# Feed-forward block on one core: a second Strassen level for product 4 of block 0, its result added to the stored rows by accumulating DMA

One core of one Trainium2 chip. The metric is the device time of one execution in microseconds (us), as the median of several runs; lower is better.

## The reference

```python
batch, m, k, h, n = 16, 512, 768, 3072, 768
def reference(x, w1, b1, w2):            # all float32
    y = np.matmul(x, w1) + b1
    y = 0.5 * y * (1.0 + erf(y / np.sqrt(2.0)))
    return np.matmul(y, w2)
```

The 8192 rows are worked in eight blocks of 1024. Each matmul is done in float16 by a Strassen-Winograd scheme: 7 products of half-size matrices in place of 8, with sums of operands made beforehand (VectorE, "DVE") and sums of products afterwards (DVE and ScalarE, "ACT"). TensorE ("PE") does the matmuls. Transfers between the chip's memory and DRAM (DMA) are issued from the queues of SyncE ("SP", the sync queue), ScalarE and GpSimd ("POOL"). "Nested" products apply the same scheme once more, so that one product becomes 7 sub-products of half the rows, half the inner dimension and half the columns.

## The kernel before

Blocks 0 and 1 do the second matmul mostly by plain products; blocks 2 to 7 do it nested throughout, with W2 operands that blocks 0 and 1 have computed and stored to DRAM (`w2s`) on the way: some as plain blocks of W2 ("raw"), most as sums of two blocks ("W2 sums"). In block 0, four units (`Unit2`, 128 row pairs each) do products 1, 3, 4, 5, 6, 7 plain, and one nested unit (`UnitH`) does product 2 for all rows. Four nested units follow each other, (0,2), (1,1), (1,4), (1,2) as (block, product), then four "lean" units of block 1.

```python
class Unit2:
    def mm(self, p, dst, first, c0, c1):
        if p == 2 or self.lean and p in (1, 4):        # these are nested
            return
        ...
        for c in range(c0, c1):                        # 12 matmuls of 384 columns
            nc.tensor.matmul(out=dst[:, 0:N2], lhsT=a, rhs=w[:, :, c, :], ...)
    def left_done(self, row, bank):
        if row == 0:
            if not self.lean:                          # upper left half: kept on chip for product 2
                nc.scalar.copy(out=self.rows(par02), in_=bank[:, 0:N2])
            return
        ...

class UnitH(Unit3):
    def __init__(self, g, sb, m):
        ...
        self.add = {0: par02, 1: par1}[self.sb] if self.p == 2 else None   # added by DVE
    def mm(self, q, dst, first, c0, c1):
        for c in range(NQ):                            # 6 x 2 matmuls of 192 columns
            for t in range(2):
                nc.tensor.matmul(out=dst[:, t * N4:(t + 1) * N4], lhsT=a, rhs=self.w[q][:, c, :], ...)

def split_w2(p, t, q=None):       # four W2 sums of product p into buffers spare[t], each then stored
    ...
            tt(t[n], a, b, SUB)                                    # DVE
            puts.append([LAG[0], lambda eng: put(n, t[n], eng)])   # store two slots later (SP queue)
```

The instruction streams are interleaved by hand: a period runs the first products of unit i and the last ones of unit i-1, with seven slots between them in which DVE work and transfers are put. DVE takes its instructions in the order of the program, so one that waits holds up those behind it (for 3.6 us in the result below).

```python
def fill_mm2_one(sb, U, slot):                         # block 0, unit U
    ...
        if U == 0:
            for p in (1, 2, 3, 5, 6, 7, 4):
                raw_w2(p)                              # 3 raw W2 tiles each, stored two per slot
            for p, t in ((6, (0, 1, 2, 3)), (1, (4, 5, 0, 1)), (4, (2, 3, 4, 5)), (2, (0, 1, 2, 5))):
                split_w2(p, t)
def fill_hyb(sb, m, slot):                             # nested units
    ...
    if m == 1 and slot == 6:
        split_w2(7, (6, 7, 8, 9))
        split_w2(5, (6, 7, 8, 9))
```

## Time and profile before

| | before |
|---|---|
| median of 3 runs | 852.22 us (851.93 to 852.35) |
| span of the profiled run | 850.3 us |
| PE instructions | 6468 matmuls and 6468 weight loads |
| first matmul of block 0's units to the first full unit of block 2 ("the stretch") | 120.53 to 230.23 us: 109.70 us |
| end of PE's last matmul to the end of the span ("the tail") | 3.75 us |

What bounds the kernel is shown in the prediction below. First the busy time of each engine in two windows, then how many W2 sums and raw tiles are stored in each (count, size, median us from issue to landing):

```profile
core 0: us, PE busy (x) PEld busy (x) DVE busy (x) ACT busy (x) POOL busy (x), PEclk, DMA share, GB/s
120.50:158.00 37.50, 37.50 (x229) 22.31 (x228) 33.18 (x46) 9.95 (x21) 0.00 (x0) 1.00 0.81 280
158.00:232.00 74.00, 74.00 (x617) 54.97 (x616) 55.48 (x80) 16.30 (x35) 13.30 (x24) 1.00 0.84 234
```

```profile
w2s<-arena SPq DMA_DIRECT2D x30, 288.0 KB, 3.8
...
w2s<-arena SPq DMA_DIRECT2D x13, 288.0 KB, 6.2
```

On average the transfers have about a fifth of the time to spare in both windows, but from 180 to 210 us their share is already 1.01 to 1.17 (three windows of 10 us). And these are the transfers of the last 10 us:

```profile
out_dram<-arena SPq DMA_DIRECT2D x5, 384.0 KB, 2.5
out_dram<-arena SPq DMA_DIRECT2D x1, 192.0 KB, 2.4
...
out_dram<-arena ACTq DMA_DIRECT2D x1, 96.0 KB, 2.3
```

### The profile page before, as it was taken

The numbers are of one execution on the slowest core, as the hardware profiler recorded it, in microseconds if no ns is written. First come the engines' busy times: TensorE is split into PE (matmuls) and PEld (weight loads), VectorE is DVE, ScalarE is ACT, GpSimd is POOL, SyncE is SP. The second block draws the span as 40 slices with busy tenths as digits, with TensorE's granted clock in tenths as the row PEclk, the third lists the DMA queues.
The fourth block names the chain that finished last, engine by engine and source line by source line (L and its number), as shares of the span: only waits on it lengthen the run. The fifth ranks groups of instructions, "written<-read, shape, count | busy, mean of one in ns | idle before, by whom it ended". The sixth has DMA issues, their size and how long they took to land.

```text
span 850.3 us, 16583 instructions
## 1 busy us (share of the span) xinstructions
PE 843.9 (99%) x6468; PEld 571.3 (67%) x6468; DVE 671.1 (79%) x1132; ACT 423.6 (50%) x692; POOL 89.9 (11%) x147
## 2 busy tenths in 40 slices
PE   8999999999999999999999999999999999999998
PEld 5444445697544897449964499645995469944798
DVE  5766679877757998679976799667996689956998
ACT  4777762221277413773147822587216771277611
POOL 5021100022200002000020000200002100010000
PEclk9999999999999999999999999999999999999999
DMA  9998697679899699977999689995999949984398
GB/s 226 193 281 182 159 194 256 232 203 262 314 278 207 199 336 363 307 166 246 337 372 283 134 287 335 373 286 112 314 345 349 293 102 331 354 312 170 101 303 290
DMA packets 144066, 220.82 MB, mean 260 GB/s; under 512 B 61916, under 2 KB 84884, under 8 KB 143988
## 3 DMA queue, kind: packets, MB, share of 16 engines
q1 hardware_dynamic: 117536, 178.36, 67.0%
q0 software_dynamic: 26272, 41.30, 21.7%
q8 instruction: 50, 0.82, 0.4%
q14 instruction: 28, 0.23, 0.1%
q10 hardware_dynamic: 180, 0.11, 0.0%
HBM read 182.07 MB, written 47.87 MB: 270 GB/s over the span
## 4 chain that ended last, share of the span: by engine, by line
PE 98%; DMA 1%; ACT 0%; DVE 0%; SPq 0%; issue 0%; ACTq 0%
PE bY L411 21%; PE bY L516 15%; PE bX L411 14%; PE bX L516 10%; PE bW L411 7%; PE bZ L411 7%; PE bZ L516 5%; PE bW L516 5%; PE bY L456 5%; PE bZ L456 2%; PE bW L456 2%; PE bY L603 1%; PE bX L603 1%; PE bX L456 1%; DMA arena<-in_x_dram 1%; PE bX L778 0%
## 5 line engine op out<-in xcount | busy, mean ns | idle before, releaser
L208 DVE TENSOR_TENSOR arena<-arena 128x1536 f16<-128x1536 f16 (+6 forms) x634 | 405.9, 671 | 6.6 <-PE bW L456 1.0
L411 PEld LDWEIGHTS <-arena 128*128 128x128 f16 x1974 | 192.5, 98 | 224.3 <-issue 0.6
L516 PEld LDWEIGHTS <-arena 128*128 128x128 f16 x3528 | 292.1, 98 | 8.3 <-issue 0.4
L411 PE MATMUL bY<-arena 128*128 128x512 f16 x846 | 214.4, 379 | 0.1
L629 DVE TENSOR_TENSOR arena<-bY,arena 128x512 f32<-128x512 f32 (+1 forms) x102 | 69.4, 680 | 119.0 <-PE bY L411 91.9
L516 PE MATMUL bY<-arena 128*128 128x192 f16 x1500 | 138.3, 246 | 0.0
L411 PE MATMUL bX<-arena 128*128 128x512 f16 x564 | 138.2, 379 | 0.0
L622 ACT COPY bY<-bX 128x512 f32<-128x512 f32 (+1 forms) x144 | 79.1, 549 | 118.2 <-DVE arena L565 81.5
L427 ACT ACTIVATE arena<-arena,b1t 128x1024 f16<-128x1024 f32 x94 | 108.0, 1149 | 52.0 <-DVE arena L657 52.0
L642 ACT COPY arena<-bW 128x512 f32<-128x512 f32 (+1 forms) x148 | 81.5, 551 | 92.2 <-PE bW L516 44.3
L516 PE MATMUL bX<-arena 128*128 128x192 f16 x1020 | 93.1, 246 | 0.1
L657 DVE TENSOR_TENSOR arena<-bZ,arena 128x512 f32<-128x512 f32 (+1 forms) x102 | 69.2, 679 | 22.1 <-PE bZ L411 18.2
L411 PE MATMUL bZ<-arena 128*128 128x512 f16 x282 | 76.2, 379 | 0.0
L411 PE MATMUL bW<-arena 128*128 128x512 f16 x282 | 76.2, 379 | 0.0
L548 POOL DMA_DIRECT2D out_dram<-arena x42 | 30.5, 728 | 409.1 <-DVE arena L653 375.0
L432 ACT ACTIVATE arena<-bX,b1t 128x512 f16<-128x512 f32 x94 | 64.0, 681 | 10.5 <-PE bX L411 10.5
L673 ACT COPY bZ<-bY 128x512 f32<-128x512 f32 (+1 forms) x58 | 30.8, 532 | 75.6 <-PE bY L456 30.0
L456 PEld LDWEIGHTS <-arena 128*128 128x128 f16 x480 | 46.9, 98 | 31.0 <-issue 0.2
L432 ACT ACTIVATE arena<-bY,b1t 128x512 f16<-128x512 f32 x94 | 63.4, 674 | 0.0
L516 PE MATMUL bZ<-arena 128*128 128x192 f16 x504 | 48.5, 246 | 0.0
L516 PE MATMUL bW<-arena 128*128 128x192 f16 x504 | 48.4, 246 | 0.0
L316 POOL DMA_DIRECT2D arena<-in_x_dram x60 | 32.3, 546 | 152.3 <-DMA arena<-arena 142.0
(62 smaller groups left out, 413.9 us busy)
## 6 DMA issues: line engine op xcount, KB each, us to landing
arena<-w2s SPq DMA_DIRECT2D x300, 288.0 KB, 4.6
arena<-w1s SPq DMA_DIRECT2D x72, 672.0 KB, 7.0
out_dram<-arena POOLq DMA_DIRECT2D x46, 384.0 KB, 7.4
w2s<-arena SPq DMA_DIRECT2D x49, 288.0 KB, 4.1
arena<-in_x_dram POOLq DMA_DIRECT2D x60, 192.0 KB, 7.3
w1s<-arena SPq DMA_DIRECT2D x12, 672.0 KB, 6.1
arena<-in_w_dram POOLq DMA_DIRECT2D x17, 384.0 KB, 7.5
out_dram<-arena SPq DMA_DIRECT2D x9, 384.0 KB, 2.6
```

The source lines that it names most:

```text
L208: nc.vector.tensor_tensor(out=o, in0=a, in1=b, op=op)
L316: nc.gpsimd.dma_start(out=xhs[t], in_=xr[:, sb * 8 + t, :])
L411: nc.tensor.matmul(out=dst[:, 0:RH], lhsT=w1_op(self.wt, slot)[:, c, :], rhs=a[:, c, :], start=first and c == 0, stop=c == self.C - 1, ski ...
L427: nc.scalar.activation(out=self.G[1][:, hi, :, :], in_=self.tmp, func=GELU, bias=b1t[:, 2 * hi + 1:2 * hi + 2])
L432: nc.scalar.activation(out=self.G[0][:, hi, row, :], in_=bank[:, 0:RH], func=GELU, bias=b1t[:, 2 * hi:2 * hi + 1])
L456: nc.tensor.matmul(out=dst[:, 0:N2], lhsT=a, rhs=w[:, :, c, :], start=first and c == 0, stop=c == self.C - 1, skip_group_check=True)
L516: nc.tensor.matmul(out=dst[:, t * N4:(t + 1) * N4], lhsT=a, rhs=w[:, c, :], start=first and c == 0 and t == ts[0], stop=c == NQ - 1, skip_ ...
L622: nc.scalar.copy(out=bY[u.g % 2][:, 0:u.F], in_=bX[u.g % 2][:, 0:u.F])
L629: nc.vector.tensor_tensor(out=u.c22(), in0=bY[u.g % 2][:, 0:u.F], in1=w[:, 0:u.F], op=ADD)
L642: nc.scalar.copy(out=w[:, 0:u.F], in_=bW[:, 0:u.F])
L657: nc.vector.tensor_tensor(out=u.c12(), in0=bZ[:, 0:u.F], in1=w[:, 0:u.F], op=ADD)
L673: nc.scalar.copy(out=bZ[:, 0:u.F], in_=bY[u.g % 2][:, 0:u.F])
```

## The change

The intent: nest product 4 of block 0 as well, which saves an eighth of its columns. Both nested products of block 0 then add to rows that the plain units have stored already: their partial sums go out by an accumulating DMA, so no DVE add is needed. The operand sums of product 4 need a place, so buffers move, and the order of the W2 sums changes. Cut to its core:

```diff
-    o_stage = o_wt + 2 * N + PAR
+    o_stage = o_wt + PAR
...
-    hyb_w = {2: {7: stage[0], 5: stage[1], 6: stage[2], 4: stage[5]}, ...
+    w4 = {7: stage[6], 5: stage[4], 6: stage[5], 4: wb_at(o_x0 + W2_N)}
+    hyb_w = [{7: stage[3], 5: stage[0], 6: stage[1], 4: stage[2]}, w4, w4,
+             {7: stage[0], 5: stage[1], 6: stage[2], 4: stage[3]},
+             {7: stage[6], 5: stage[4], 6: stage[5], 4: stage[1]}]
...
-        HYBRID = ((0, 2), (1, 1), (1, 4), (1, 2))
+        HYBRID = ((0, 2), (0, 4), (1, 4), (1, 1), (1, 2))
...
-                if p == 2 or self.lean and p in (1, 4):
+                if p in (2, 4) or self.lean and p == 1:
...
             def finish(self):
...
+                    if self.sb:
+                        nc.gpsimd.dma_start(out=o, in_=d)
+                    else:
+                        nc.gpsimd.dma_start(out=o, in_=d, accum_op=ADD)
...
         def fill_mm2_one(sb, U, slot):
-                    for p, t in ((6, (0, 1, 2, 3)), (1, (4, 5, 0, 1)), (4, (2, 3, 4, 5)), (2, (0, 1, 2, 5))):
-                        split_w2(p, t)
-            drain(slot)
+                    w4 = (6, 4, 5, 3)
+                    split_w2(4, w4, ns=(5, 6, 4))
+                    split_w2(1, (0, 1, 2, 6))
+                    split_w2(2, (3, 0, 1, 2))
+                    split_w2(4, w4, ns=(7,))
+            drain(slot, 3 if U == 0 and slot > 1 else 0)
...
         def fill_hyb(sb, m, slot):
-            drain(slot)
+            drain(slot, int(slot > 1))
...
+            if m == 2 and slot == 1:
+                load_w2s(3, (5, 6, 7, 4))
+            if m == 3 and slot == 1:
+                load_w2s(4, (5, 6, 7))
+            if m == 4 and slot == 1:
+                load_w2s(4, (4,))
+            if m == 2 and slot == 5:
+                for p in (6, 7):
+                    split_w2(p, (7, 8, 9, 10))
...
         def fill_lean(sb, k, slot):
-                split_w2(3, (1, 2, 3, 4))
+                for p in (5, 3):
+                    split_w2(p, (0, 2, 3, 5))
```

More of the change, by code (lines that the diff above doesn't have):

```diff
@@ L164 @@
           for o in (o_x0 + W2_N, o_x0 + W2_N + GS_N, o_x1, o_x1 + GS_N)]
-    osbs = [[cut(o, n).bitcast(FP32) for o, n in zip(oo, (2 * N2, 2 * N))]
-            for oo in ((o_x1 + 2 * GS_N + 2 * N + 2 * N2, o_wt),
-                       (o_x1 + 2 * GS_N + 2 * N, o_x1 + 2 * GS_N))]
-    assert 2 * N + 4 * N2 <= PAR
-    par02, par1, par4 = [cut(o, PAR).bitcast(FP32).rearrange(
-        "p (r t h n) -> p r t h n", r=2, t=2, h=2) for o in (o_wt + 2 * N, 2 * XT_N, o_x1 + 2 * GS_N)]
+    osbs = [[cut(o + a * 2 * N, 2 * N).bitcast(FP32) for a in range(2)]
+            for o in (o_wt, o_x1 + 2 * GS_N)]
+    par02, par04, par1, par4 = [cut(o, PAR).bitcast(FP32).rearrange(
+        "p (r t h n) -> p r t h n", r=2, t=2, h=2)
+        for o in (o_wt, o_x1, 2 * XT_N, o_x1 + 2 * GS_N)]
     par11 = cut(o_w2, W2P).bitcast(FP32).rearrange("p (c n) -> p c n", c=NH)[:, 0:8, 0:N4].rearrange(
@@ L180, in wb_at @@
         return cut(off, WB, "p (c n) -> p c n", c=NQ)
-    hyb_lev = [[strip(0, 0, 0, 0), strip(1, 1, 0, 0), Gs[0][1][:, 0:NQ, 0, 2 * P:RH], strip(1, 1, NQ, 0)],
-               [strip(0, 1, 0, 0), strip(0, 0, NQ, 0), strip(0, 1, NQ, 0), strip(0, 0, 0, 2 * P)],
-               [strip(0, 1, 0, 2 * P), strip(0, 0, NQ, 2 * P), strip(0, 1, NQ, 2 * P), strip(0, 0, 0, 0)],
-               [strip(0, 1, 0, 0), strip(0, 0, NQ, 0), strip(0, 1, NQ, 0), strip(0, 0, NQ, 2 * P)]]
+    S = [strip(0, a, c, r) for r in (0, 2 * P) for c in (0, NQ) for a in range(2)]
+    hyb_lev = [[S[0], S[1], Gs[0][1][:, 0:NQ, 0, 2 * P:RH], S[2]],
+               [S[3], S[4], Gs[0][1][:, 0:NQ, 1, 2 * P:RH], S[6]],
+               [S[5], S[7], S[0], S[1]],
+               [S[2], S[3], S[4], S[6]],
+               [S[5], S[0], S[7], S[2]]]
     spare = stage + [wb_at(2 * XT_N + o) for o in
@@ L189 @@
     assert XT_N + 2 * WB + 5 * K == GR // 2
-    hyb_w = {2: {7: stage[0], 5: stage[1], 6: stage[2], 4: stage[5]},
-             1: dict(zip((7, 4, 5, 6), map(wb_at, (o_x0 + W2_N, o_x0 + W2_N + WB, o_x1, o_x1 + WB)))),
-             4: {7: wb_at(o_x1), 4: wb_at(o_x1 + WB), 5: stage[3], 6: stage[4]}}
+    w4 = {7: stage[6], 5: stage[4], 6: stage[5], 4: wb_at(o_x0 + W2_N)}
+    hyb_w = [{7: stage[3], 5: stage[0], 6: stage[1], 4: stage[2]}, w4, w4,
+             {7: stage[0], 5: stage[1], 6: stage[2], 4: stage[3]},
+             {7: stage[6], 5: stage[4], 6: stage[5], 4: stage[1]}]
     b1t = wp.tile([P, 2 * NH], FP32, name="b1t")
@@ L266, in quarters, with split_w2 @@
             return w[:, 0, 0:NQ, :], w[:, 1, 0:NQ, :], w[:, 0, NQ:NH, :], w[:, 1, NQ:NH, :]
-        def split_w2(p, t, q=None):
+        def split_w2(p, t, q=None, ns=(7, 5, 6, 4)):
             b11, b12, b21, b22 = quarters(p)
@@ L279, in f, with load_w2s @@
                     puts.append([LAG[0], lambda eng: put(n, t[n], eng)])
-                later(WB, f, slow if q is None else q)
-        def load_w2s(p, qs):
+                if n in ns:
+                    later(WB, f, slow if q is None else q)
+        def load_w2s(m, qs):
             for q in qs:
-                nc.sync.dma_start(out=hyb_w[p][q], in_=w2s[p, q][:])
+                nc.sync.dma_start(out=hyb_w[m][q], in_=w2s[HYBRID[m][1], q][:])
         def raw_w2(p):
@@ L357 @@
                    5: GA, 6: GB, 7: G1[:, :, 1, :]}
-        HYBRID = ((0, 2), (1, 1), (1, 4), (1, 2))
+        HYBRID = ((0, 2), (0, 4), (1, 4), (1, 1), (1, 2))
         def operand(sb, p):
-            return OPERAND[p] if sb else Gs[0][1][:, :, 0, :]
+            return OPERAND[p] if sb else Gs[0][1][:, :, p // 4, :]
         def half_sums(c, ks=(0, 1, 2)):
@@ L442, in __init__ @@
                 self.lean = sb > 0
-                self.eng = nc.gpsimd if self.lean else nc.sync
                 self.o = osbs1[u - NU] if self.lean else osbs[u % 2]
             def mm(self, p, dst, first, c0, c1):
-                if p == 2 or self.lean and p in (1, 4):
+                if p in (2, 4) or self.lean and p == 1:
                     return
@@ L452, in mm @@
                 for c in range(c0, c1):
-                    a = {1: G1[:, c, 0, r], 4: G2[:, c, 1, r],
-                         3: GS[3][:, c, :], 5: GS[0][:, c, :], 6: GS[1][:, c, :],
+                    a = {1: G1[:, c, 0, r], 3: GS[3][:, c, :], 5: GS[0][:, c, :], 6: GS[1][:, c, :],
                          7: GS[2][:, c, :]}[p]
@@ L466, in c12 @@
             def c12(self):
-                return self.o[0]
+                return self.o[0] if self.lean else self.o[0][:, N2:N]
             def c22(self):
@@ L472, in right_done @@
             def right_done(self):
-                self.eng.dma_start(out=orr[:, self.sb * 8 + self.u, N2:N], in_=self.o[0])
+                nc.gpsimd.dma_start(out=orr[:, self.sb * 8 + self.u, N2:N], in_=self.o[0]) if self.lean else \
+                    nc.sync.dma_start(out=orr[:, self.sb * 8 + self.u, :], in_=self.o[0])
             def left_done(self, row, bank):
-                if row == 0:
-                    if not self.lean:
-                        nc.scalar.copy(out=self.rows(par02), in_=bank[:, 0:N2])
+                if self.lean and row == 0:
                     return
@@ L482, in left_done @@
                 else:
-                    nc.scalar.copy(out=self.o[1][:, 0:N2], in_=bank[:, 0:N2])
-                self.eng.dma_start(out=orr[:, self.sb * 8 + NU + self.u, :], in_=self.o[1])
+                    nc.scalar.copy(out=self.o[row][:, 0:N2], in_=bank[:, 0:N2])
+                if row == 1:
+                    eng = nc.gpsimd if self.lean else nc.sync
+                    eng.dma_start(out=orr[:, self.sb * 8 + NU + self.u, :], in_=self.o[1])
         units3 = {}
@@ L586, in __init__ @@
                 self.g, (self.sb, self.p) = g, HYBRID[m]
-                self.lev, self.w = hyb_lev[m], dict(hyb_w[self.p])
+                self.lev, self.w = hyb_lev[m], dict(hyb_w[m])
                 b11, _, b21, b22 = quarters(self.p)
                 self.w.update({1: b11, 2: b21, 3: b22})
-                self.add = {0: par02, 1: par1}[self.sb] if self.p == 2 else None
-                self.dst = {1: par1, 4: par4, 2: par11}[self.p] if self.sb else par02
+                self.add = par1 if self.sb and self.p == 2 else None
+                self.dst = {(0, 2): par02, (0, 4): par04, (1, 1): par1, (1, 4): par4,
+                            (1, 2): par11}[self.sb, self.p]
                 self.alloc = lambda: None
@@ L608, in finish @@
             def finish(self):
-                if self.p == 2:
-                    for n in range(NU):
-                        nc.gpsimd.dma_start(
-                            out=orr[:, self.sb * 8 + n, 0:N2].rearrange("p (h n) -> p h n", h=2),
-                            in_=self.dst[:, n // 2, n % 2])
+                if self.sb and self.p != 2:
+                    return
+                for n in range(NU):
+                    o = orr[:, self.sb * 8 + self.p // 4 * NU + n, 0:N2].rearrange(
+                        "p (h n) -> p h n", h=2)
+                    d = self.dst[:, n // 2, n % 2]
+                    if self.sb:
+                        nc.gpsimd.dma_start(out=o, in_=d)
+                    else:
+                        nc.gpsimd.dma_start(out=o, in_=d, accum_op=ADD)
         def p1(u, c0, c1):
@@ L946, in fill_mm1, with drain @@
                 flush(soon)
-        def drain(slot, eng=nc.sync, wait=True):
+        def drain(slot, n=0, eng=nc.sync, wait=True):
             for f in puts:
@@ L952, in drain @@
                 puts.pop(0)[1](eng)
-            if slot > 1:
-                for f in raws[:2]:
-                    f()
-                del raws[:2]
+            for f in raws[:n]:
+                f()
+            del raws[:n]
         def fill_mm2_one(sb, U, slot):
@@ L983, in fill_mm2_one @@
                 lev_sums(None, m=0, ks=(2,))
-            if U + 1 == NU and slot == 2:
-                lev_sums(None, m=1, ks=(0, 1, 2))
             if slot > 1:
@@ L996, in fill_hyb @@
         def fill_hyb(sb, m, slot):
-            drain(slot)
+            drain(slot, int(slot > 1))
             if m == 0 and slot == 1:
-                load_w2s(1, (7, 4))
-                lev_sums(None, m=1, ks=(3,))
-            if m == 0 and slot == 4:
-                load_w2s(1, (5, 6))
-            if m == 0 and slot == 5:
-                lev_sums(None, m=2)
-            if m == 1 and slot == 5:
-                lev_sums(None, m=3, ks=(0, 1))
-            if m == 1 and slot == 6:
-                split_w2(7, (6, 7, 8, 9))
-                split_w2(5, (6, 7, 8, 9))
-            if (m, slot) in ((1, 6), (2, 1), (2, 3), (2, 5), (3, 1), (3, 5)):
-                slow.pop(0)[1]()
-            if m == 2 and slot == 1:
-                load_w2s(4, (7, 4))
-                lev_sums(None, m=3, ks=(2,))
-            if m == 2 and slot == 5:
-                lev_sums(None, m=3, ks=(3,))
-            if m == 3 and slot == 2:
+                load_w2s(1, (4,))
+                lev_sums(None, m=1)
+            if m == 0 and slot == 6:
+                lev_sums(None, m=2)
+            if m == 2 and slot == 1:
+                load_w2s(3, (5, 6, 7, 4))
+                lev_sums(None, m=3, ks=(0, 1, 2))
+            if m == 2 and slot == 4:
+                lev_sums(None, m=3, ks=(3,))
+            if m == 3 and slot == 1:
+                load_w2s(4, (5, 6, 7))
+                lev_sums(None, m=4, ks=(0, 1, 2))
+            if m == 3 and slot == 4:
+                lev_sums(None, m=4, ks=(3,))
+            if m == 4 and slot == 1:
[3 more added lines that the diff above has]
+                    split_w2(p, (7, 8, 9, 10))
+            if slow and (m == 2 or slot in (1, 4, 6)):
+                slow.pop(0)[1]()
+            if m == 4 and slot == 2:
                 for k in (0, 1):
@@ L1023, in fill_hyb @@
                 flush(queue)
-                if m == 1:
+                if m == 2:
                     load_next_x(2, range(5))
-                if m == 3:
+                if m == 4:
                     for t in range(3):
```

## The prediction

> **What bounds the kernel now.** I read the page first, then what PE waited for, then the chain that ended last in order of time, and last VectorE (DVE) in the stretch that is edited. From the page:
>
> ```profile
> PE 843.9 (99%) x6468; PEld 571.3 (67%) x6468; DVE 671.1 (79%) x1132; ACT 423.6 (50%) x692; POOL 89.9 (11%) x147
> ...
> PE 98%; DMA 1%; ACT 0%; DVE 0%; SPq 0%; issue 0%; ACTq 0%
> ```
>
> PE holds 98% of the chain. A busy PE can still be badly fed, so I asked for its waits alone (total us, times, longest):
>
> ```profile
> PE bX L756 <- DVE arena L742: 1.2, 1, 1.2
> PE bT L330 <- DVE arena L762: 1.1, 2, 0.9
> ```
>
> These are the only rows: 2.3 us, all in the prologue. After it PE never waited for a sum, an eviction, a bank or a weight. So time leaves only with matmul columns, and comes back only if some new wait reaches PE. The chain in order of time (start us, us, what) gives the price of a product in both forms:
>
> ```profile
> 144.09 1.95 PE bW L456 x12
> 146.04 1.95 PE bZ L456 x12
> 147.99 3.90 PE bY L456 x24
> ...
> 184.29 1.98 PE bY L603 x24
> 186.27 1.98 PE bX L603 x24
> ```
>
> Line 456 is the plain second-matmul product of one 128-row unit: 12 matmuls of 384 columns in 1.95 us, 162.5 ns each. Line 603 is the nested product: 24 matmuls of 192 columns in 1.98 us, 82.5 ns each, so 0.99 us for one of its seven sub-products (12 matmuls). The starts follow without a gap. (The 326 and 246 ns that the groups give for one matmul are latencies that overlap, and must not be added.)
>
> [...] one sum of 128x1536 lasts 0.95 us, three in a row 2.69 us, so 0.87 us is the step. [...] The kernel before has no accumulating DMA, so its trace cannot confirm the cost.
>
> **The change part by part.**
>
> *Matmuls, the only term on the path.* Product 4 of block 0's second matmul was plain in four units: 4 x 12 matmuls, 4 x 1.95 = 7.80 us. It becomes a fifth nested unit: 7 sub-products x 0.99 = 6.93 us, 84 matmuls instead of 48 (36 more instructions, 6468 to 6504). Difference: **-0.87 us**, 0.10% of 852.22. Product 2 was nested already. No other matmul changes.
>
> *DVE, beside PE.* One more nested unit needs four level sums of 128x1536: 4 x 0.87 = +3.5 us. Its two evictions (lines 627 and 653, 0.55 us long, step 0.47) add 0.9. The add of the stored half is no longer done in the nested unit of product 2: its four DVE adds (lines 646, 670 and 565 twice) go, 4 x 0.47 = -1.9. The number of W2 sums (4 for each of 7 products) is the same, only their order differs. Net about +2.5 us of DVE in the stretch from 120 to 231 us, which has room as a sum; whether it has room at each deadline is the first rival below.
>
> *ScalarE, beside PE.* Three copies for product 2 (in place of the adds) and five for product 4: 8 x 0.47 = +3.8 us; it is busy under a third of that stretch.
>
> *DMA, beside PE.* The row-0 stores of the four units grow from 192 KB to 384 KB: +0.8 MB. Four plain 192 KB stores become accumulating ones and four are added: +0.8 MB[...]. Reloaded W2 operands go from 6 to 9 tiles of 288 KB: +0.9 MB. That is some 4 MB on 221. The raw W2 stores move: 15 of 21 go out in the first unit, then the rest in the nested units, instead of ten, ten and one. From 120.5 to 132 us the DMA share is 0.52, from 144 to 156 it is 1.00, so the move levels the load.
>
> *Shape of the stretch.* Units of block 0 shrink from 11.70 us (six products) to 9.75 (five), and the first nested period from 9.81 to 7.86. Four nested units of 6.93 then follow instead of three. All of block 0 before that, blocks 1 to 7 and the tail keep their instructions, so a saving here is carried to the end unchanged.
>
> **The rivals.**
>
> *1. DVE too late in the first nested period.* Here the change is tightest: its period issues eight level sums (four of the second nested unit, four of the third), where before there were five. Counting from the period's start: the eviction after the last unit's product 7 can start at 2.94 + 0.25 us (that lag is what the trace shows at 166.37 to 166.62) and ends at 3.66; two sums to 5.40; the next eviction waits for product 3 (5.88 + 0.2) and ends at 6.55; six sums of 0.87 to 11.8; the next unit's first eviction to 12.3. PE needs that bank for its sub-product 4 at 7.86 + 4.95 = 12.81. So the margin is about 0.4 us[...]. DVE does not come in late: here is the same place before, with almost three us of idle DVE ahead of it:
>
> ```profile
> 160.20 3.55 DVE L208 TENSOR_TENSOR arena<-arena 128x1536 f16<-128x1536 f16 x4
> 166.62 0.56 DVE L629 TENSOR_TENSOR arena<-bY,arena 128x384 f32<-128x384 f32 x1 [2.87 <-issue]
> ```
>
> The later nested periods carry at most four level sums, three W2 sums and two to five evictions, some 6 to 6.9 us in 6.93. DVE may trail by 1 to 2 us, but its results there are wanted a period later. If I misjudge this, PE waits 0.2 to 1 us: 851.6 to 852.4.
>
> *2. The accumulating DMA holds a buffer.* The partial sums of product 4 lie where the third and fourth operand sums of block 1's units go (two times 12x128 elements, exactly the 3072 of the partial). DVE may write there only when the accumulating stores have read it. They can be issued some 6 us into the third nested period; the overwriting sum comes 22 us into it. A plain GpSimd store of this size lands in:
>
> ```profile
> out_dram<-arena POOLq DMA_DIRECT2D x12, 192.0 KB, 4.0
> ```
>
> Even at an estimated three times that, 12 us, there are about 4 us to spare, and DVE waiting a little is not yet PE waiting. Against it: five loads of x and the W2 stores share these queues, with a DMA share of about 1 from 179 us on. A bad case costs 1 to 4 us: 852.5 to 855.
>
> *3. Reloaded W2 operands late.* Tiles of products (1,1) and (1,2) now all come from DRAM. Their buffers come free so early that the loads can be issued 8 us or more before use, against a landing time of 4.6 us; before, the margin was nearer 3 us and PE did not wait. The stages also move down by 1536 elements, so that the last W2 stores share bytes with a weight tile of block 2; that load (7.0 us) is needed some 13 us after its issue. Little chance, cost up to 2 us.
>
> *4. A larger gain,* by relief of DVE or DMA: excluded, since PE waits for neither today.
>
> **Range and chances.** 852.22 - 0.87 = 851.35, given as 851.4. The three runs before spread over 0.4 us, so 0.2 of noise each way is granted. I give about 75% to no new wait at all, 15% to under 1 us of it, 10% to more; this skews the range upward: 850.9 to 852.1. Two per cent would be 17 us: faster is impossible, as all of product 4 costs 7.8 us; slower would need a wait repeated in every later block, or a DMA far slower than I assume.
>
> **What would show it.** Right: 6504 matmuls; PE waits only the two prologue rows; units of 9.75 us and five nested units of 6.93; everything after about 230 us shifted earlier by 0.87. Wrong: a row of PE waiting for line 627 (rival 1), of DVE line 208 waiting for a DMA into the output (rival 2), or of PE's weight loads or matmuls waiting for a W2 or w1 load (rival 3). A stretch without such a row that still isn't shorter would overthrow the pricing itself.

(The forecast of time is 852.22 - 0.87 = 851.35: the 1.95 and 0.99 us behind its 7.80 and 6.93 are read from the chain it prints. Of the transfers, "some 4 MB" counts a term of 1.6 MB for reading back; the other parts come to 2.5 MB, and the pages show 2.47 MB more moved, 220.82 and 223.29. What the halves cost beside the columns is the difference of the two steps in the forecast: two nested matmuls of 82.5 ns against one plain one of 162.5, 2.5 ns more. That 0.87 us is an upper value for a DVE sum was not shown: in the changed kernel two in a row took 1.94 us, so the step there was 0.99.)

## The result

| | before | changed |
|---|---|---|
| median | 851.91 us (851.56 to 852.35, 6 runs) | 857.22 us (856.15 to 858.57, 6 runs) |
| ratio of the fast runs | | 1.0063 (1.005 to 1.0076) |
| span of the profiled run | 850.3 us | 855.3 us |
| stretch | 109.70 us | 113.86 us |
| tail | 3.75 us | 5.12 us |

The time lies 5.1 us above the upper end of the forecast range (852.1), though still within 2% of before. (All line numbers of the changed kernel differ: 606 is the nested matmul, 457 the plain one, 210 the DVE sums.)

PE's waits in the changed kernel, total us, times, longest:

```profile
PE bY L606 <- DVE bZ L678: 3.3, 1, 3.3
PE bX L764 <- DVE arena L750: 1.2, 1, 1.2
PE bT L333 <- DVE arena L770: 1.0, 1, 1.0
```

One new row: a nested matmul waited 3.3 us for a DVE instruction. The chain of what released what, in order of time (start us, us, what), shows what stood behind it:

```profile
181.14 0.56 DVE arena L635
181.70 0.95 DVE arena L210 x2
182.65 9.58 DMA w2s<-arena
192.23 0.02 issue
192.25 0.04 DVE arena L210
...
195.59 0.57 DVE bZ L678
196.16 0.04 issue
196.20 2.08 PE bY L606 x12
198.28 2.65 PE bW L457 x12
```

Read it from the bottom. PE waited for the add of line 678, which stood behind other DVE work; DVE had stood still until 192.23, 3.6 us by its own list of waits, for a store of a W2 sum to DRAM. That store took 9.58 us from issue to landing. The link is a buffer: the sums of product 6 and of product 7 share four buffers (`split_w2` for 6 and 7, both into 7 to 10), and a sum of product 7 may not be written before product 6's has been read out. DVE works in order, so an evicting add (one that empties a result bank for PE's next product) waited with it.

The last two rows hold a second loss. After 3.3 us of idleness the 12 nested matmuls took 2.08 us instead of 0.99, and the next 12 took 2.65 instead of 1.95: 1.79 us more, with a granted clock of 0.50 from 196.2 to 198.2 us and 0.76 to 201.0. In finer windows it is 0.50 up to 199.5 us and 1.00 from 199.6 on, some 3.4 us after PE went on. The length of the wait alone did not decide it. From start to start the 12 nested matmuls took 1.88 us here after 3.27 us of idle PE, and 1.87 in a run below (the x loads) after 2.91, but 0.99 in another (no accumulation) after 3.50. (The ends of matmuls are modelled in these traces; the weight loads stood still for 3.42, 3.05 and 3.65 us in the three cases.)

So the stretch adds up: -0.87 (the saved columns) + 3.27 (wait) + 1.79 (clock) = +4.19, measured 113.86 - 109.70 = +4.16. The rest of the 5.0 us of the span lies in the tail, +1.37, less 0.39 by which the profiled run reached the stretch earlier and 0.14 after it.

Why did the store take 9.6 us? The first suspicion was the order of the W2 stores. The same windows and stores as before:

```profile
120.50:158.00 37.50, 37.50 (x234) 22.60 (x233) 33.08 (x46) 10.28 (x22) 0.00 (x0) 1.00 0.64 230
158.00:232.00 74.00, 70.72 (x627) 55.76 (x625) 54.20 (x76) 17.74 (x39) 17.61 (x26) 0.98 0.99 258
```

```profile
w2s<-arena SPq DMA_DIRECT2D x21, 288.0 KB, 4.1
...
w2s<-arena SPq DMA_DIRECT2D x21, 288.0 KB, 4.3
```

Nine W2 stores have left the first window, whose DMA share fell from 0.81 to 0.64, and eight more are in the second, whose share rose from 0.84 to 0.99. (The median of 4.3 us hides the late ones: the seven stores issued between 170 and 200 us have a median landing of 9.5, the seven reloads 7.9.) Whether this shift is what made the store late is tested below; it turns out not to be ("Both").

And the tail. These are the last 11 us; the first line is a fetch of instructions, which the same window did not have before:

```profile
q8 instruction: 1, 0.02, 0.5%
...
out_dram<-arena SPq DMA_DIRECT2D x5, 384.0 KB, 3.4
out_dram<-arena SPq DMA_DIRECT2D x1, 192.0 KB, 3.6
out_dram<-arena ACTq DMA_DIRECT2D x1, 96.0 KB, 3.1
```

The same last stores land about a microsecond later.

### The profile page after: what moved, and what is told of

Its sections match the earlier page's. It is cut to its first block, busy times and chain, and to the rows that moved or that the text cites. A ratio compares the mean times of both kernels' runs of the same rounds, so it can differ in the third digit from the quotient of the medians.

```text
span 855.3 us, 16683 instructions
## 1 busy us (share of the span) xinstructions
PE 844.6 (99%) x6504; PEld 574.6 (67%) x6504; DVE 673.1 (79%) x1134; ACT 426.6 (50%) x700; POOL 95.1 (11%) x151
## 2 busy tenths in 40 slices
DMA packets 145395, 223.29 MB, mean 261 GB/s; under 512 B 62028, under 2 KB 85508, under 8 KB 145316
## 4 chain that ended last, share of the span: by engine, by line
PE 96%; DMA 2%; DVE 1%; issue 0%; SPq 0%; ACT 0%; ACTq 0%
PE bY L414 21%; PE bY L518 15%; PE bX L414 14%; PE bX L518 10%; PE bW L414 7%; PE bZ L414 7%; PE bZ L518 5%; PE bW L518 5%; PE bY L457 4%; PE bW L457 2%; PE bZ L457 2%; PE bY L606 1%; DMA w2s<-arena 1%; PE bX L457 1%; PE bX L606 1%; DMA arena<-in_x_dram 1%
```

## The experiments

All kernels give a correct result unless it is said otherwise. Edits are against the changed kernel unless it is said otherwise. The theories: A, the accumulating stores make every transfer slow; B, the order in the sync (SP) queue makes the store late; C, the traffic as a whole; later D, the moved W2 stores fill the second half; E, the instruction fetch in the tail.

### No accumulation

```diff
-                        nc.gpsimd.dma_start(out=o, in_=d, accum_op=ADD)
+                        nc.gpsimd.dma_start(out=o, in_=d)
```

> Wrong result on purpose: the eight stores of the nested partial sums overwrite instead of accumulating; everything else is the changed kernel. Theory A (the accumulating stores slow all transfers of the stretch, so that the store of a W2 sum, 9.6 us to landing, comes too late for its buffer to be written again): the wait of DVE for that store and PE's wait of 3.3 us go, the clock stays full, and the time falls to about 851.0 (before 851.9 less 0.87). Theory B (the store is late because the sync queue issues it behind three loads that wait for PE): PE's wait stays at 3 us or falls by under 1 us, time 855 to 857. Theory C (the traffic as a whole, x loads and reloads of W2, fills the queues): about half, 853 to 856.

Result wrong. 858.69 us (857.65 to 863.09), ratio 1.0083 (1.0056 to 1.011). DVE's wait in the nested units:

```profile
DVE arena L210 <- DMA w2s<-arena: 3.8, 1, 3.8
```

No shorter than before the edit, although the GpSimd stores of 192 KB between 158 and 206 us, the eight among them, land in 4.1 us instead of 7.0. Theory A falls as the whole cause. The profile is of its slowest run, 863 us: PE waited twice more in it, in block 1's units and for a W1 tile. After the first wait, of 3.50 us, the next 12 nested matmuls took their usual 0.99 us.

### Product 7's sums later

```diff
-            if slow and (m == 2 or slot in (1, 4, 6)):
+            if len(slow) > 4 and (m == 2 or slot in (1, 4, 6)):
...                                                   # in fill_lean
-            if slow and slot in (2, 5):
+            if slow and slot in (2, 4, 5):
-            if k == 1 and slot == 2:                  # W1 tiles whose place the late sums need
+            if k == 1 and slot == 6:
```

> The four W2 sums of product 7, which write the buffers of product 6's sums again, run in block 1's units instead of the nested units; the transfers of the nested stretch stay except these four stores, the accumulating stores stay. If the wait of DVE for that one buffer is the whole cause, whatever makes the store slow: PE waits only in the prologue, time 850.8 to 851.4, faster than before by 0.1%. If the slow transfers hurt elsewhere too, a wait appears at another place and the time stays above 852.

860.69 us (859.35 to 864.8), ratio 1.0104 (1.0076 to 1.0133). The wait in the nested units is gone, as expected of taking away the second use of the buffer there; but the time did not come back. DVE stands before the same kind of buffer some 30 us later, one that products 5 and 3 share and whose sums the edit packs three to a unit instead of two:

```profile
227.67 0.76 DVE L210 TENSOR_TENSOR arena<-arena 128x1152 f16<-128x1152 f16 x1 [8.61 <-DMA w2s<-arena]
```

and PE waits 6.7 us. The store in question took 8.2 us to land. So it is not that one buffer: in both kernels DVE waits where a buffer is to be written again sooner than its store lands.

### Reloads behind the stores

```diff
-            if m == 3 and slot == 1:
-                load_w2s(4, (5, 6, 7))
+            if m == 3 and slot == 3:
+                load_w2s(4, (5, 6, 7))
```

> The three reloads for the last nested unit are issued two slots later, so that the stores of product 6's sums are no longer behind them in the sync queue. Theory B (order in the queue): the store goes out some 2.6 us earlier, DVE waits under 1 us instead of 3.6, PE does not wait or under 0.7 us, time 851 to 853. Theory A or C alone: the store lands as late as before, since the 16 engines are full, PE waits over 2 us, time 855 to 857.

858.91 us (858.14 to 861.15), ratio 1.008 (1.0063 to 1.0097). DVE no longer waits for a store, so the order in the queue does decide who is late, as B says; but now the reload is:

```profile
PE bW L606 <- DMA arena<-w2s: 3.7, 1, 3.7
```

B moves the wait and does not remove it: 3.7 us instead of 3.3.

### The x loads later

```diff
-                if m == 2:
+                if m == 3:
                     load_next_x(2, range(5))
```

> The five x loads of block 2 go out one nested period (6.9 us) later. Theory C (x loads fill the queues while the store is under way): the store lands in 5 to 7 us instead of 9.6, DVE waits under 1 us, time 851 to 853, unless the x transposes then come late. Theory A: little change, PE waits 2 us or more, 854 to 857.

857.62 us (857.09 to 857.88), ratio 1.0061. Not conclusive: the edit did nothing. The GpSimd queue is ahead of PE and nothing held these loads back, so they went out at 180 to 184 us as before. Here the place in the program did not set when the transfers started.

### The raw W2 stores back in the first units

```diff
-            drain(slot, 3 if U == 0 and slot > 1 else 0)
+            drain(slot, 3 if U < 2 and slot > 1 else 0)
```

> The last six raw W2 stores go out in the second unit, where the DMA share was 0.43, instead of in the first two nested units. Theory D (the new program moves W2 stores out of the half-idle stretch before 158 us into the full one after it: 30 stores before 158 us and 13 after it became 21 and 21): the backlog is smaller, but these six had landed by 170 us, so little of it is theirs; the critical store lands 0 to 2 us earlier, PE still waits 1.5 to 3.3 us, time 854 to 857. If the raw stores are the main culprit, the wait goes and the time is near 851.

857.57 us (857.2 to 859.4), ratio 1.0062 (1.0045 to 1.0078). DVE waited 4.7 us, PE 4.3. The DMA share from 160 to 170 us fell from 0.89 to 0.44, but from 180 to 190 it is 1.09 as before. Load taken away before the jam did not shorten it: the store that DVE waited for took 10.4 us to land. (That what follows is paced by PE, and so cannot start earlier, is a likely reason; no run tests it.)

### Product 6's sums back in the first units

```diff
                     w4 = (6, 4, 5, 3)
+                    split_w2(6, (0, 1, 2, 6))
...
-                for p in (6, 7):
-                    split_w2(p, (7, 8, 9, 10))
+                split_w2(7, (7, 8, 9, 10))
```

> Product 6's four W2 sums and stores go back to the first units, as in the kernel before; the nested units keep product 7's four alone and no buffer is written twice there. Theory D with the buffer as its point of contact: no wait of DVE for a W2 store in the nested units, four stores fewer in the full stretch, the reloads for the last nested unit land in 5 to 7 us instead of 8.8, PE waits only in the prologue: 850.8 to 851.6, faster than before by 0.1%. If the stretch stays too full, a wait for a reload or in block 1's units takes its place: 852 to 856.

852.28 us (851.96 to 856.67), ratio 1.0013 (0.9988 to 1.0037). The wait in the nested units is gone and 5 us come back, although the second store of a sum there still takes 10.1 us to land. It is not quite enough: the profiled run was the longest one, of 856.67 us, with DVE waiting 1.6 and 3.3 us for W2 stores in block 1's units and PE 2.5.

### Both

> Both of the above: ten W2 stores back before 158 us. Theory D: no wait of PE, 850.8 to 851.5, and a smaller spread between runs than with either part alone. The rival (the accumulating stores by themselves fill the queues, wherever the W2 stores are): still 853 or more.

852.74 us (852.48 to 853.48), ratio 1.0008 (0.9993 to 1.0023). All of PE's waits:

```profile
PE bX L764 <- DVE arena L750: 1.2, 1, 1.2
PE bY L414 <- DVE bZ L683: 0.4, 1, 0.4
PE bT L333 <- DVE arena L770: 0.2, 1, 0.2
```

The stretch takes 108.83 us against 109.70: the 0.87 us of the prediction, to the digit. 32 W2 stores lie before 158 us (DMA share 0.85) and 12 after. All accumulating stores are still there, so the rival in the expectation falls. But the time is not 851: the tail is 5.47 us.

Theory D, as the reason why a store lands late, falls with this run too: the second half is as full as in the changed kernel (share 0.97 against 0.99; from 180 to 190 us 1.11 against 1.09), and the stores land no faster. This is the second store of a W2 sum in the nested units, issued at about 183 us, the one that DVE waited for: before, changed, both.

```profile
w2s<-arena SPq DMA_DIRECT2D x1, 288.0 KB, 8.3
w2s<-arena SPq DMA_DIRECT2D x1, 288.0 KB, 9.6
w2s<-arena SPq DMA_DIRECT2D x1, 288.0 KB, 9.5
```

What differs is when its buffer is written again. Before, that was 10.2 us after the store's issue (183.67 to 193.92), 1.9 us after it had landed. In the changed kernel DVE came to it 6.0 us after (182.65 to 188.64) and had to wait. With product 6's sums back in the first units, no buffer of W2 sums is written twice in the nested units at all. So the repair takes away the second write; it does not relieve the transfers.

### No x loads

```diff
-                    load_next_x(2, range(5))
+                    for t in range(5):
+                        xhs[t] = xh_of(2, t)
```

> Wrong result on purpose: the five x loads of block 2 in the nested stretch (landing 12 us) are left out, nothing else. The earlier attempt to move them later did not move them, since the GpSimd queue runs ahead of PE. Theory C (the x loads, 1.97 MB read, are what holds up the store of the W2 sum): the store lands in 4 to 6 us, DVE does not wait, time about 851. If the sync queue's own eight transfers in a row are enough to hold it up: it lands in 7 us or more, and PE waits 1 us or more, 853 or more.

Result wrong. 856.95 us (852.75 to 860.83), ratio 1.0055 (1.0012 to 1.0097). DVE's wait in the nested units is halved, 1.8 us instead of 3.6, and PE's is 1.5; the profiled run then waited in block 1's units. The store that DVE waited for landed in 7.3 us instead of 9.6. The x loads are a part of the jam, about half of the wait by this one profile, and not all of it. (The runs spread over 8 us and the profile is of the slowest.)

### The tail: more PE instructions in the kernel before

The edit is against the kernel before, in its warm-up:

```diff
-                nc.tensor.matmul(out=(bX[1], bY[1])[k % 2][:], lhsT=zero[:, 0, 0:P], rhs=zero[:, 0, :], ...)
+                for c in range(4):
+                    cc = slice(c * P, (c + 1) * P)
+                    nc.tensor.matmul(out=(bX[1], bY[1])[k % 2][:, cc], lhsT=zero[:, 0, 0:P], rhs=zero[:, 0, cc], ...)
```

> The kernel before, with each of its 17 warm-up matmuls of 512 columns written as four of 128: the same columns, 102 PE instructions more. Theory E (the tail: PE fetches its instructions in pieces of 16 KB, one about every 11 us; with 72 more instructions than before the last fetch falls within the last us of PE's work and the last stores and the end of the kernel come later): one fetch more (51 instead of 50), it falls 2 to 3 us before PE's end, the time from PE's end to the end of the span grows from 3.75 to 5 us or more, time 853.3 to 853.9 against 852.2. Rival (the tail has to do with the accumulating stores or the W2 traffic): tail 3.75, time as before within 0.3.

854.34 us (854.06 to 854.98), ratio 1.0028 (1.0016 to 1.0041). The last fetch lies at 846.5 to 847 us, about a microsecond before PE's end; before, the last one was at 838.2, 8 us before it. The tail grew from 3.75 to 4.88 us, with no change to any store:

```profile
q8 instruction: 1, 0.02, 0.5%
...
out_dram<-arena SPq DMA_DIRECT2D x1, 192.0 KB, 3.7
out_dram<-arena SPq DMA_DIRECT2D x1, 96.0 KB, 3.4
```

(The page of the changed kernel counts 51 fetches and 0.84 MB, so 16 KB each; its last five lie near 806, 817, 828, 837 and 849 us.) So the tail depends on where the last fetch falls (3.75 us at 838.2, 4.88 at 846.5 to 847), and that on how many instructions PE has (102 more here). Of the rest of the 2.3 us by which the span grew, 0.32 lie between the stretch and PE's end and 0.85 at the start: PE reached the stretch later, in this run with a wait for x; in the next experiment it is 0.87 later than in its control, so cutting up the warm-up matmuls seems to cost that.

### The tail: the same edit in the repaired version

> The repaired version (six raw W2 stores and product 6's sums back in the first units) with the same split of the warm-up matmuls. Theory E: the last fetch moves from 0.6 us before PE's end to about 5 us before it, ahead of the last stores, so the tail is 3.6 to 4.2 us instead of 5.47, time 851.0 to 851.6, which beats the kernel before by 0.6 to 1.2 us. Rival: tail still 5.2 to 5.5, time 852.5 or more.

852.92 us (852.09 to 853.16), ratio 1.0009 (0.9997 to 1.0022). The last fetch lies at 841 us, 6 us before PE's end, the stores land quickly again, and the tail is 3.74 us:

```profile
out_dram<-arena SPq DMA_DIRECT2D x5, 384.0 KB, 2.5
out_dram<-arena SPq DMA_DIRECT2D x1, 192.0 KB, 2.3
```

Theory E holds in both directions. The time I expected did not come: 0.87 us at the start, and PE waited 1.5 us for a reload for the last nested unit.

### Control

> The repaired version again, unchanged, as the control for the run with split warm-up matmuls on the same chip: 852.4 to 853, tail 5.3 to 5.5 us, the stretch of the second matmul of blocks 0 and 1 shorter than before by 0.87 us again.

852.51 us (851.92 to 855.01), ratio 1.0014 (1.0001 to 1.0028). Stretch 108.83 us again, tail 5.07. One run in five was at 855.01, unprofiled; a wait may still come back at times, which no trace shows.

### A version meant to beat both

Against the repaired version: the reloads go out as soon as their buffers are free, and 63 matmuls of block 2 are written as two of 256 columns.

```diff
+            if m == 2 and slot == 6:
+                load_w2s(4, (5, 6))
+            if m == 3 and slot == 3:
+                load_w2s(4, (4,))
             if m == 3 and slot == 1:
-                load_w2s(4, (5, 6, 7))
+                load_w2s(4, (7,))
-            if m == 4 and slot == 1:
-                load_w2s(4, (4,))
...                                                   # Unit1.mm
+                parts = (slice(0, RH // 2), slice(RH // 2, RH)) if self.sb == ONE and self.k < 3 else (slice(0, RH),)
+                    for r in parts:
+                        nc.tensor.matmul(out=dst[:, r], ..., rhs=a[:, c, r], start=first and c == 0 and r.start == 0, ...)
```

> Attempt at a version that beats both: the repaired version, plus the reloads for the last nested unit issued as soon as their buffers come free (two of them before the stores of product 7's sums, the fourth a period earlier), plus 63 matmuls of 512 columns in the first three units of block 2 written as two of 256 (126 PE instructions more[...]), so that the last instruction fetch falls some 5 us before PE's end. The warm-up matmuls stay whole, since splitting them seems to have cost some 0.8 us at the start. If all three findings hold (PE work -0.87, late reloads, last fetch): stretch 108.8, tail 3.7 to 4.0, no wait of PE after the prologue, time 851.0 to 851.6, faster than before by 0.3 to 1 us. If the stretch is still too full: a wait of 1 to 2 us in one run or the other, median 852 or more.

851.45 us (851.33 to 851.74) against 852.03 (851.67 to 852.22) for the kernel before, ratio 0.9995 (0.9981 to 1.0008). PE waits 1.9 us in all, 1.6 of them in the prologue. The tail is 3.80 us, the last fetch at 838 us. Over all 14 profiles: in the eleven whose last fetch falls in about the last microsecond of PE's work the tail is 4.9 to 5.5 us, in the three where it falls 6 to 8 us earlier 3.7 to 3.8. It is the fastest of all versions by its median, 0.58 us below before and 5.8 below the change as given; the interval does not exclude that it equals the kernel before.

## Why the prediction was wrong

**The pricing was right.** Product 4 nested saves 0.87 us of PE: the stretch of 108.83 us in two profiles (the repaired version and its control) shows it, and the sum of the changed kernel's stretch closes with it. Rival 1 did not happen: PE never waited in the first nested period. That eviction ended 12.4 us into it, where I had estimated 12.3 and PE needed it at 12.81.

**The step that failed is in the DVE part:** "The number of W2 sums [...] is the same, only their order differs", and, of the later nested periods, "DVE may trail by 1 to 2 us, but its results there are wanted a period later". I counted DVE's work there, and not what it might have to wait for: four buffers that the sums of two products share. In the new order DVE came to write such a buffer again 6.0 us after its store was issued, instead of 10.2, where a store takes 9.6 us to land (8.3 before). DVE stood still for 3.6 us and PE for 3.3. Taking away the second write there takes PE's wait away, while the store lands as late as ever.

**The DMA part was wrong too, but is not shown to be the cause.** I counted bytes over the whole kernel and the raw stores alone, and wrote "so the move levels the load". It did the opposite: product 6's four stores and some raw ones moved behind 158 us, 30 and 13 W2 stores became 21 and 21, and the shares went from 0.81 and 0.84 to 0.64 and 0.99. But the transfers from 180 us on were full before the change already, and putting ten stores back did not make them faster. For rival 3 I used 4.6 us for a reload; in the second window the reloads land in 7.3. They were in time in the changed kernel, but 1.5 us late in the repaired one with split warm-up matmuls, and 3.7 us late when I delayed them.

**The point of contact was not on my list.** I looked at what the accumulating stores hold (rival 2) and at the W2 reloads (rival 3), not at the stores of the sums. The wait I named as a sign of rival 2, DVE line 208 waiting for a DMA into the output, did not appear; it waited for a DMA into `w2s`.

**The cost of a wait was mis-sized.** I allowed up to 4 us for a bad case. A wait of 3.27 us cost 5.06, because the granted clock was 0.50 after it.

**The tail "keeps its instructions", but not its time.** I took the end for untouched, and counted 36 more PE instructions where it is 72 with the weight loads. Adding them shifts the last instruction fetch into the last microsecond of PE's work: +1.37 us, shown by adding instructions to the kernel before (+1.13) and by adding more to the repaired version (-1.33 against its control). With this term even a change without any wait would have come out at about 852.4 (851.91 - 0.87 + 1.37), above my upper bound; the repaired version ran at 852.74 and 852.51.

**What stays open.** How one fetch of 16 KB makes all last stores about 1 us slower is not settled. The traces give a hint: in the kernel before, the last transfers stop at once, while with the late fetch (changed kernel, repaired one, kernel before with more instructions) they fade out at 20 to 28 GB/s for 0.8 to 1.5 us, about a sixteenth of the 350 GB/s just before. The fetch itself took 0.5% of 16 engines' time in 11 us, an estimated 0.9 us of one engine. One of the 16 engines being late with its part of the last stores would fit both; that is a guess, which no run tests. Why a store takes 8 to 10 us to land near 183 us is only bounded: without x loads it took 7.3 in one profile, without accumulation 10.2, with the raw stores moved away 10.4, and an attempt to move the x loads failed to move them.

## What to carry to other kernels

When PE never waits, price the saved columns from the chain. Then make a second ledger for the buffers that are written twice: from the issue of the store that reads one to its next write, against the landing time in that very window, not the median of the whole kernel (9.6 us here against 4.1). Giving a store more time, or its buffer a single use, can cure such a wait without the transfers getting any faster (9.5 us to land in the repaired version, and no wait for it); undoing one such wait alone may move it to the next (6.7 us of PE, some 30 us later, in one run). A wait of PE of 3.27 us cost half as much again here, 1.79 us, through a granted clock of 0.50; the same matmuls were as slow after 2.91 us, and not after 3.50. And look at what falls into the last ten microseconds: the tail went from 3.75 to 5.12 us though its code is untouched.
